# A decoder layer's two norms: GpSimd takes the residual and the bias, ScalarE the normalising, and the first norm's statistics are formed in another way

## The chip, the cores and the metric

The kernel runs on one core of a Trainium2 chip. The engines are called PE (TensorE, the matrix engine; PEld is its loading of weights), DVE (VectorE), ACT (ScalarE), POOL (GpSimd) and SP (SyncE, which here only issues transfers). The metric is the device time in microseconds (us) of one execution; the median of three runs is quoted.

## The reference, cut to what matters

One layer: a token mixer, a residual with a norm, a mixture of experts, a residual with a norm. There are T = 2048 tokens of D = 1024 features. Only the two norms and the sum of the experts matter here:

```
x = layer_norm(ALPHA * x + g1 * (mixed @ w_out), ln_mix_g, ln_mix_b)     # first norm
h = x * (1 + sc2) + sh2
y = routed_experts(h) + swiglu(h, sh_w1, sh_w3, sh_w2)                   # 64 experts and a shared one
x = layer_norm(ALPHA * x + g2 * y, ln_ffn_g, ln_ffn_b)                   # second norm, the output

layer_norm(x, g, b): (x - mean) * rsqrt(mean((x - mean)^2) + 1e-5) * g + b     # per token
```

## The kernel before, in words

Tokens lie on the 128 partitions, so a block is 128 tokens by 1024 features in float32, and there are 16 blocks. Matrix products are made of three products of split operands (high and low part). The instructions of each engine run in the order that a planner (a list scheduler with priorities and assumed costs) wrote down when the kernel was built; an engine never passes over a waiting instruction. DMA issues of one engine wait in the same way, in the order of its queue.

**The first norm** (phase_c, L1755 to L1985). For each of 16 blocks PE multiplies the mixer's output with w_out into two PSUM tiles of 512 columns (48 matmuls, L1836). DVE forms r = ALPHA * x + product from each half (L1837) and the half's mean and variance sums (bn_stats, L1840). layer_norm_hat (L1988) joins the two (bn_aggr, L1996), makes the reciprocal root with small DVE instructions (rsqrt, L711 to L716: two integer steps and three Newton steps of three instructions) and has ACT write (r - mean) * rstd (L2004). DVE then makes h2 (L1845, L1849) and x1, the normed stream, already multiplied by ALPHA (L1851, L1852); both go to HBM. PE transposes h2 (L1860), ACT copies it out (L1861), PE forms the router's scores (L1865), and DVE picks the experts.

**The experts and the last stage** (moe_phase). First the shared expert's output for blocks 0 to 5 is written to a buffer acc in HBM; then the routed experts add their outputs to acc by indirect transfers that POOL issues (L2166). When the last of them has landed, the last stage runs: for blocks 6 to 15, in four units of two blocks and two of one, PE computes the shared expert (hidden, L2112 and L2093, and back, L2129). finish (L2353) does one block per step. sums (L2344) loads x1 into y (L2347) and acc into a (L2349), both on SP's queue, and DVE multiplies a by g2 (L2350). back first adds y to the PSUM tile by a matmul with the identity matrix (L2126, two halves per block). DVE then reads the PSUM tile, adds a, and sums the row on the way (L2371). Blocks 0 to 5 need no matmul: in each of the first six steps one of them is taken along, and DVE adds y and a in two halves (L2366).

**The second norm** (norm, L2320) works on one or two blocks at a time: DVE the mean (L2327), ACT the sum of squares (L2329), DVE the variance (L2332) and rsqrt, then per block two instructions of DVE, (y - mean) * ln_g (L2339) and * rstd + ln_b (L2340), and the transfer to the output (L2341, SP's queue). The tiles `y` come from a ring of 8, `a`, the loaded h2 and the scratch of the squares from a ring of 6 (xg).

The lines of the second norm that the change touches:

```
V.scalar_tensor_tensor(y[:, hs], y[:, hs], mean[:, i:i + 1], ln[0][:, hs], op0=ALU.add, op1=ALU.mult)
V.scalar_tensor_tensor(y[:, hs], y[:, hs], rs[:, i:i + 1], ln[1][:, hs], op0=ALU.mult, op1=ALU.add)
nc.sync.dma_start(out[rows, hs], y[:, hs])
```

Of the kernel before, what the change touches and what calls it, by code (L numbers as in the profile page):

```python
# [6 lines left out]
F32 = mybir.dt.float32  # L7
# [5 lines left out]
AF = mybir.ActivationFunctionType  # L13
ALU = mybir.AluOpType
AX = mybir.AxisListType
PSUM = bass.MemoryType.PSUM
P = 128
T = 2048
D = 1024
KT = D // P  # L20
NT = T // P
CH = 512
# [6 lines left out]
ALPHA = 2.0 ** 0.25  # L29
# [1725 lines left out]
def phase_c(tc, A, g, S, mixT, modrow, C):  # L1755


    nc = tc.nc
    V, G, ACT, PE = nc.vector, nc.gpsimd, nc.scalar, nc.tensor
    woH, woL = C.wo  # L1760
    with ExitStack() as es:
# [3 lines left out]
        wk = pool("c_wk", 2)  # L1765
# [52 lines left out]
        def tile_(t, h2T):  # L1818
            t0 = t * P
            parts = C.first if t == 0 else []  # L1820
            load = mixed(nc, S, mx_ if t % 2 else C.mx, t, parts, G if t == 1 else nc.sync, V)
            if t:
                next(load)
            x = xp.tile([P, D], F32, name="x")
            nc.sync.dma_start(x, A["x"][0, t0:t0 + P, :])
            if t:
                next(load)
            mH, mL = parts
            yield
            r = rp.tile([P, D], F32, name="r")  # L1830
            for n in range(2):
                ps = C.pp.tile([P, CH], F32, name="po")
                sl = slice(n * 512, (n + 1) * 512)
                for k in range(KT):
                    for i, (a_, b_) in enumerate(((mH, woH), (mH, woL), (mL, woH))):
                        PE.matmul(ps, lhsT=a_[:, k, :], rhs=b_[:, k, sl], start=(k == 0 and i == 0), stop=(k == KT - 1 and i == 2))  # L1836
                V.scalar_tensor_tensor(r[:, sl], x[:, sl], ALPHA, ps, op0=ALU.mult, op1=ALU.add)  # L1837
                if n == 0:
                    st = sm.tile([P, 2, 6], F32, name="lnst", bufs=2)
                V.bn_stats(out=st[:, n, :], in_=r[:, sl])  # L1840
                yield
            xh = layer_norm_hat(tc, sm, r, r, st=st)
            yield
            h2 = wk.tile([P, D], F32, name="h2")
            V.tensor_tensor(h2, xh, bc["sc2"], op=ALU.mult)  # L1845

            hp = wk.tile([P, D], F32, name="h2p", bufs=3)
            cut = lambda a: a.rearrange("p (q k) -> p q k", k=KT)
            V.tensor_tensor(hp.rearrange("p (k q) -> p q k", k=KT), cut(h2), cut(bc["sh2"]), op=ALU.add)  # L1849
            h2 = hp  # L1850
            V.tensor_tensor(xh, xh, lng, op=ALU.mult)  # L1851
            V.tensor_tensor(xh, xh, lnb, op=ALU.add)  # L1852
            nc.sync.dma_start(S["x1"][t0:t0 + P, :], xh)
            nc.sync.dma_start(S["h2"][t0:t0 + P, 0:D], h2)
            yield
            hT = wk.tile([P, KT, P], F32, name="hT")
            for n in range(2):
                ps = pt.tile([P, CH], F32, name="tr")
                for k in range(4):
                    PE.transpose(ps[:, k * P:(k + 1) * P], h2[:, (4 * n + k) * P:(4 * n + k + 1) * P], g.ident)  # L1860
                ACT.activation(hT[:, 4 * n:4 * n + 4, :].rearrange("p a b -> p (a b)"), ps, AF.Copy)  # L1861
            yield
            ps = pr.tile([P, CH], F32, name="rt")
            for k in range(KT):
                PE.matmul(ps[:, 0:NE], lhsT=hT[:, k, :], rhs=rw[:, k, :], start=(k == 0), stop=(k == KT - 1))  # L1865
            ACT.activation(h2T, ps[:, 0:NE], AF.Sigmoid)
            yield
# [117 lines left out]
        rank_experts(tc, g, S, cnt_e, sm, pr)  # L1985


def layer_norm_hat(tc, sm, out, r, parts=1, st=None):  # L1988

    nc = tc.nc  # L1990
    if st is None:
        st = sm.tile([P, 2, 6], F32, name="lnst")
        for n in range(2):
            nc.vector.bn_stats(out=st[:, n, :], in_=r[:, n * 512:(n + 1) * 512])
    mv = sm.tile([P, 2], F32, name="lnmv")
    nc.vector.bn_aggr(out=mv, in_=st)  # L1996
    va = sm.tile([P, 1], F32, name="lnva")
    nc.vector.tensor_scalar(va, mv[:, 1:2], 1e-5, None, op0=ALU.add)
    y = rsqrt(nc, sm, va, [P, 1], None, "ln")
    nb = sm.tile([P, 1], F32, name="lnnb")  # L2000
    nc.vector.scalar_tensor_tensor(nb, mv[:, 0:1], -1.0, y, op0=ALU.mult, op1=ALU.mult)
    for i in range(parts):
        c = slice(i * D // parts, (i + 1) * D // parts)
        nc.scalar.activation(out[:, c], r[:, c], AF.Identity, bias=nb, scale=y)  # L2004
    return out
NEAR = 4
NEAR2 = 5
# [6 lines left out]
def moe_phase(tc, A, g, S, modrow, out):  # L2014
    nc = tc.nc
    V, G, ACT, PE = nc.vector, nc.gpsimd, nc.scalar, nc.tensor
    with ExitStack() as es:
# [100 lines left out]
                V.tensor_tensor(s[:, 0:n], s[:, 0:n], ps[1][:, 0:n], op=ALU.mult)  # L2118
                split_to(nc, gH[:, m, 0:n], gL[:, m, 0:n], s[:, 0:n])

        def back(w, gH, gL, c, n, more=None):

            for h in range(2):
                ps = py_.tile([P, CH], F32, name="py")
                if more is not None:
                    PE.matmul(ps, lhsT=g.ident, rhs=more[:, h * CH:(h + 1) * CH], start=True, stop=False)  # L2126
                for m in range(2):
                    for j, (a, b) in enumerate(TERMS):
                        PE.matmul(ps[:n], lhsT=(gH, gL)[a][:, m, c:c + n], rhs=w[2][b][:, m, h * CH:(h + 1) * CH],  # L2129
                                  start=(more is None and m == 0 and j == 0), stop=(m == 1 and j == 2))  # L2130
                yield h, ps

        def gather(idx, eid, c0, n):
# [186 lines left out]
        def norm(blocks):  # L2320


            n = len(blocks)
            mean = sm.tile([P, 2], F32, name="lnmean")[:, 0:n]
            sq = sm.tile([P, 2], F32, name="lnsq")[:, 0:n]
            for i, (rows, y, su) in enumerate(blocks):
                V.tensor_scalar(mean[:, i:i + 1], su[:, 0:1], su[:, 1:2], -1.0 / D, op0=ALU.add, op1=ALU.mult)  # L2327
                junk = xg.tile([P, HC], F32, name="x")[:, 0:D]
                ACT.activation(junk, y, AF.Square, bias=mean[:, i:i + 1], accum_out=sq[:, i:i + 1])  # L2329
            yield  # L2330
            va = sm.tile([P, 2], F32, name="lnva")[:, 0:n]
            V.tensor_scalar(va, sq, 1.0 / D, 1e-5, op0=ALU.mult, op1=ALU.add)  # L2332
            rs = rsqrt(nc, sm, va, [P, n], None, f"ln{n}")
            yield
            for i, (rows, y, su) in enumerate(blocks):
                parts = 2 if rows.stop == T else 1
                for q in range(parts):
                    hs = slice(q * D // parts, (q + 1) * D // parts)
                    V.scalar_tensor_tensor(y[:, hs], y[:, hs], mean[:, i:i + 1], ln[0][:, hs], op0=ALU.add, op1=ALU.mult)  # L2339
                    V.scalar_tensor_tensor(y[:, hs], y[:, hs], rs[:, i:i + 1], ln[1][:, hs], op0=ALU.mult, op1=ALU.add)  # L2340
                    nc.sync.dma_start(out[rows, hs], y[:, hs])  # L2341
                yield

        def sums(rows):  # L2344

            y = buffer()
            nc.sync.dma_start(y, S["x1"][rows, :])  # L2347
            a = xg.tile([P, HC], F32, name="x")[:, 0:D]
            nc.sync.dma_start(a, S["acc"][rows, :])  # L2349
            V.tensor_tensor(a, a, g2b, op=ALU.mult)  # L2350
            return y, a, sm.tile([P, 2], F32, name="lnsu", bufs=8)

        def finish(w, c0, n, g_, more):  # L2353
            done = []
            for c in range(0, n, P):
                rows = slice(c0 + c, c0 + c + P)
                y, a, su = sums(rows)
                norms()
                blocks_left[0] -= 1
                early = []  # L2360
                for _ in range(-(-len(more) // (blocks_left[0] + 1))):
                    r2 = slice(more[-1], more.pop() + P)
                    y2, a2, su2 = sums(r2)
                    for q in range(2):
                        hs = slice(q * CH, (q + 1) * CH)
                        V.scalar_tensor_tensor(y2[:, hs], y2[:, hs], 1.0, a2[:, hs], op0=ALU.mult, op1=ALU.add,  # L2366
                                               accum_out=su2[:, q:q + 1])
                    done.append((r2, y2, su2))
                for q, ps in back(w, g_[0], g_[1], c, P, y):
                    hs = slice(q * CH, (q + 1) * CH)  # L2370
                    V.scalar_tensor_tensor(y[:, hs], ps, 1.0, a[:, hs], op0=ALU.mult, op1=ALU.add, accum_out=su[:, q:q + 1])  # L2371
                done.append((rows, y, su))
                if len(done) >= 2 or c + P == n:
                    for i in range(0, len(done), 2):
                        under_way.append(norm(done[i:i + 2]))
                        next(under_way[-1])
                    done = []
                yield
# [115 lines left out]
```

## Time and profile before

| what | us |
|---|---|
| median of three runs (lowest, highest) | 3731.58 (3721.93, 3741.07) |
| the profiled execution, its own time | 3729.63 |
| its span, first to last instruction | 3727.9 |
| the first norm's steady stretch (from 1840 to 2010) | 170 |
| the last stage, from the first L2350 to the last DVE instruction | 102.5 |

In the rows below a time at the head of a line is counted from the span's start; the second figure is the instruction's duration. "x2" behind a row of a timeline means that two neighbours were merged. An instruction's record can begin before its predecessor on the same engine has ended, so the distance of two starts is the better measure of what one costs in a full queue. `w` and `x` are the program's names for the tiles that hold y and a; `wraw` is the tile with ln_g or ln_b, and `py`, `tr`, `p` and `po` are PSUM tiles.

### The profile page before, as it was taken

To read this page: it belongs to the slowest core of one execution; us is meant where nothing else is said; L and a number is where in the kernel's file an instruction comes from. 1 tells how busy PE (TensorE), PEld (TensorE's weight loads), DVE (VectorE), ACT (ScalarE), POOL (GpSimd) and SP (SyncE) were. 2 spreads that over 40 slices of the span, in tenths; PEclk is the share of its full clock that TensorE was granted. 3 is DMA by queue.
4 is the path that set the end of the run, shared out by engine and by line. 5 is a ranking of instruction groups with operands and counts; after the bars stand their busy time and mean duration, and the time that the engine had idled before them with its cause. 6 is when DMAs were issued, how large, how long until landed. Compare 5 with 4: busy or idle time off the path is not lost. (4 is left out here: it accounts for less than half of the span.)

```text
span 3727.9 us, 64046 instructions
## 1 busy us (share of the span) xinstructions
PE 3439.3 (92%) x23084; PEld 2985.7 (80%) x23084; DVE 2640.9 (71%) x6951; ACT 1962.2 (53%) x3471; POOL 881.8 (24%) x817
## 2 busy tenths in 40 slices
PE   7899999799999879999898799999999999999998
PEld 5677777688888767778787798998888888888996
DVE  6555899888888678888799545555556555556659
ACT  4243656355555567767322355555555555556642
POOL 1000000322223155543000022332223322232210
PEclk9999999899999889999999899999999999999999
DMA  7756466400000132222543478888889888888986
GB/s 251 232 199 221 150 211 226 162 26 25 20 24 18 30 105 79 84 66 78 170 149 140 146 206 232 242 232 233 244 244 242 244 236 234 236 234 256 290 237 215
DMA packets 276235, 640.38 MB, mean 172 GB/s; under 512 B 34428, under 2 KB 115364, under 8 KB 275784
## 3 DMA queue, kind: packets, MB, share of 16 engines
q1 hardware_dynamic: 231760, 481.09, 38.6%
q0 software_dynamic: 40832, 150.32, 18.2%
q10 hardware_dynamic: 3320, 4.83, 0.4%
q8 instruction: 183, 3.00, 0.3%
q14 instruction: 140, 1.15, 0.1%
HBM read 467.14 MB, written 169.00 MB: 171 GB/s over the span
## 5 line engine op out<-in xcount | busy, mean ns | idle before, releaser
L2112 PE MATMUL p<-hH,w 128*128 128x256 f32 (+8 forms) x4352 | 875.1, 289 | 9.3 <-DVE w L2060 6.6
L2112 PEld LDWEIGHTS p<-hH,w 128*128 128x128 f32 x4352 | 707.4, 191 | 18.9 <-DVE w L2060 6.9
L2060 DVE TENSOR_TENSOR w<-wraw,w 128x1024 fp32r<-128x1024 f32 x396 | 474.7, 1223 | 293.2 <-ACT w L2059 278.9
L2112 PE MATMUL p<-hL,w 128*128 128x256 f32 (+8 forms) x2176 | 617.2, 284 | 0.7 <-DVE hL L65 0.7
L2059 ACT ACTIVATE w<-wraw 128x1024 fp32r<-128x1024 f32 x396 | 406.2, 1054 | 234.5 <-DMA wraw<-in_exp_w_dram 112.2
L2166 POOL DMA_INDIRECT scratch_acc<-y,idx x157 | 262.3, 1671 | 782.6 <-ACT y L2165 312.8
L2129 PE MATMUL py<-w,gH 128*128 128x512 f32 (+5 forms) x1384 | 441.8, 401 | 2.0 <-ACT gH L62 1.6
L2112 PEld LDWEIGHTS p<-hL,w 128*128 128x128 f32 x2176 | 416.4, 191 | 6.5 <-DVE hL L65 0.9
L343 PE MATMUL pj<-hTH,w 128*128 128x512 f32 x1152 | 376.6, 402 | 16.6 <-ACT w L202 10.8
L65 DVE TENSOR_TENSOR hL<-tr,hH 128x512 fp32r<-128x512 f32 (+7 forms) x346 | 213.2, 627 | 210.8 <-ACT hH L62 197.6
L2129 PEld LDWEIGHTS py<-w,gH 128*128 128x128 f32 (+5 forms) x1384 | 236.6, 178 | 68.4 <-issue 8.1
L2165 ACT ACTIVATE y<-py,gt 128x512 f32<-128x512 f32 (+5 forms) x314 | 213.6, 683 | 145.9 <-PE py L2129 132.8
L343 PEld LDWEIGHTS pj<-hTH,w 128*128 128x128 f32 x1152 | 220.5, 193 | 70.8 <-ACT w L202 13.8
L62 ACT ACTIVATE hH<-tr 128x512 fp32r<-128x512 f32 (+7 forms) x346 | 184.3, 545 | 176.1 <-PE tr L2072 156.5
L2129 PE MATMUL py<-w,gL 128*128 128x512 f32 (+5 forms) x692 | 273.9, 396 | 0.6 <-DVE gL L65 0.5
L2140 POOL DMA_INDIRECT x<-scratch_h,idx x157 | 162.9, 1038 | 333.0 <-DVE L L2182 80.3
L343 PE MATMUL pj<-hTL,w 128*128 128x512 f32 x576 | 230.9, 401 | 0.0
L2072 PE MATMUL tr<-ident,x 128*128 128x128 f32 (+5 forms) x1384 | 191.9, 265 | 35.0 <-issue 17.9
L2072 PEld LDWEIGHTS tr<-ident,x 128*128 128x128 f32 (+5 forms) x1384 | 149.6, 140 | 46.0 <-issue 30.5
L2129 PEld LDWEIGHTS py<-w,gL 128*128 128x128 f32 (+5 forms) x692 | 122.9, 178 | 39.1 <-DVE gL L65 1.8
L2093 PE MATMUL p<-w,hH 128*128 128x256 f32 (+2 forms) x736 | 141.8, 289 | 0.0
L343 PEld LDWEIGHTS pj<-hTL,w 128*128 128x128 f32 x576 | 111.5, 194 | 23.5 <-issue 0.9
(626 smaller groups left out, 8152.0 us busy)
## 6 DMA issues: line engine op xcount, KB each, us to landing
wraw<-in_exp_w_dram SPq DMA_DIRECT2D x384, 512.0 KB
w<-scratch_wH SPq DMA_DIRECT2D x57, 512.0 KB
w<-scratch_wL SPq DMA_DIRECT2D x57, 512.0 KB
mw<-in_w_mod_dram SPq DMA_DIRECT2D x48, 512.0 KB
scratch_rw<-po SPq DMA_DIRECT2D x44, 256.0 KB
w<-in_w_in_dram SPq DMA_DIRECT2D x21, 512.0 KB
x<-in_x_dram SPq DMA_DIRECT2D x40, 256.0 KB
scratch_wH<-w SPq DMA_DIRECT2D x19, 512.0 KB
```

The costliest lines, as they stand in the source:

```text
L62: nc.scalar.activation(hi, src, AF.Copy)
L65: (lo_eng or nc.vector).tensor_tensor(lo, src, hi.bitcast(F32), op=ALU.subtract)
L343: nc.tensor.matmul(ps, lhsT=a_[:, k, :], rhs=b_[k], start=(k == 0 and i == 0), stop=(k == KT - 1 and i == 2))
L2059: ACT.activation(wh[:, c], raw, AF.Copy)
L2060: V.tensor_tensor(wl[:, c], raw, wh[:, c].bitcast(F32), op=ALU.subtract)
L2072: PE.transpose(ps[:, k * n:(k + 1) * n], x[0:n, (4 * h + k) * P:(4 * h + k + 1) * P], g.ident[0:n, 0:n])
L2093: PE.matmul(ps[i][:n, 0:256], lhsT=(hH, hL)[a][:, k, 0:n], rhs=w[i][b][:, k, :], start=(k == 0 and j == 0), stop=(k == KT - 1 and j == 2))
L2112: PE.matmul(ps[i][:, 0:n], lhsT=w[i][a][:, k, m * P:(m + 1) * P], rhs=(hH, hL)[b][:, k, 0:n], start=(k == 0 and j == 0), stop=(k == KT - 1 ...
L2129: PE.matmul(ps[:n], lhsT=(gH, gL)[a][:, m, c:c + n], rhs=w[2][b][:, m, h * CH:(h + 1) * CH], start=(more is None and m == 0 and j == 0), s ...
L2140: G.indirect_dma_start(out=x[0:m, :], out_offset=None, in_=S["h2"], in_offset=bass.IndirectOffsetOnAxis(ap=ix[0:m], axis=0))
L2165: ACT.activation(y[:m, hs], ps[:m], AF.Copy, scale=gt[:m])
L2166: G.indirect_dma_start(out=S["acc"], out_offset=bass.IndirectOffsetOnAxis(ap=ix[0:m], axis=0), in_=y[0:m, :], in_offset=None, compute_op=A ...
```

## The change

In the last stage GpSimd adds y (x1) to a after DVE's product with g2. The matmul with the identity is gone. For blocks 0 to 5 ACT copies a to y in two halves and sums on the way. In the norm DVE forms -mean * rstd (nb), ACT writes y * rstd + nb, DVE multiplies by ln_g, and GpSimd adds ln_b, except in blocks 14 and 15, where DVE does. In the first norm the row sums come from L1837 itself, ACT forms the sum of squares of r - mean, and bn_stats and bn_aggr are gone.

```
@@ phase_c, tile_
-                V.scalar_tensor_tensor(r[:, sl], x[:, sl], ALPHA, ps, op0=ALU.mult, op1=ALU.add)
                 if n == 0:
-                    st = sm.tile([P, 2, 6], F32, name="lnst", bufs=2)
-                V.bn_stats(out=st[:, n, :], in_=r[:, sl])
+                    su = sm.tile([P, 2], F32, name="lnsu", bufs=2)
+                V.scalar_tensor_tensor(r[:, sl], x[:, sl], ALPHA, ps, op0=ALU.mult, op1=ALU.add, accum_out=su[:, n:n + 1])
                 yield
-            xh = layer_norm_hat(tc, sm, r, r, st=st)
-            yield
             h2 = wk.tile([P, D], F32, name="h2")
+            xh = layer_norm_hat(tc, sm, r, r, su, h2)
+            yield
@@ layer_norm_hat(tc, sm, out, r, su, junk)
-    nc.vector.bn_aggr(out=mv, in_=st)
+    mean = sm.tile([P, 1], F32, name="lnmean")
+    nc.vector.tensor_scalar(mean, su[:, 0:1], su[:, 1:2], -1.0 / D, op0=ALU.add, op1=ALU.mult)
     va = sm.tile([P, 1], F32, name="lnva")
-    nc.vector.tensor_scalar(va, mv[:, 1:2], 1e-5, None, op0=ALU.add)
+    nc.scalar.activation(junk, r, AF.Square, bias=mean, accum_out=va)
+    nc.vector.tensor_scalar(va, va, 1.0 / D, 1e-5, op0=ALU.mult, op1=ALU.add)
...
@@ back
-                if more is not None:
-                    PE.matmul(ps, lhsT=g.ident, rhs=more[:, h * CH:(h + 1) * CH], start=True, stop=False)
@@ norm
+            nb = sm.tile([P, 2], F32, name="lnnb")[:, 0:n]
+            V.tensor_tensor(nb, mean, rs, op=ALU.mult)
             yield
             for i, (rows, y, su) in enumerate(blocks):
+                ACT.activation(y, y, AF.Identity, bias=nb[:, i:i + 1], scale=rs[:, i:i + 1])
+                ended = rows.stop > T - 2 * P
                 parts = 2 if rows.stop == T else 1
                 for q in range(parts):
                     hs = slice(q * D // parts, (q + 1) * D // parts)
-                    V.scalar_tensor_tensor(y[:, hs], y[:, hs], mean[:, i:i + 1], ln[0][:, hs], op0=ALU.add, op1=ALU.mult)
-                    V.scalar_tensor_tensor(y[:, hs], y[:, hs], rs[:, i:i + 1], ln[1][:, hs], op0=ALU.mult, op1=ALU.add)
+                    V.tensor_tensor(y[:, hs], y[:, hs], ln[0][:, hs], op=ALU.mult)
+                    (V if ended else G).tensor_tensor(y[:, hs], y[:, hs], ln[1][:, hs], op=ALU.add)
                     nc.sync.dma_start(out[rows, hs], y[:, hs])
@@ sums
             V.tensor_tensor(a, a, g2b, op=ALU.mult)
+            G.tensor_tensor(a, a, y, op=ALU.add)
@@ finish
                     for q in range(2):
                         hs = slice(q * CH, (q + 1) * CH)
-                        V.scalar_tensor_tensor(y2[:, hs], y2[:, hs], 1.0, a2[:, hs], op0=ALU.mult, op1=ALU.add,
-                                               accum_out=su2[:, q:q + 1])
+                        ACT.activation(y2[:, hs], a2[:, hs], AF.Identity, accum_out=su2[:, q:q + 1])
                     done.append((r2, y2, su2))
-                for q, ps in back(w, g_[0], g_[1], c, P, y):
+                for q, ps in back(w, g_[0], g_[1], c, P):
```

## Rows read from the trace of the kernel before

**Rows 1.** Busy time by stretch: the stretch, its length, then the busy time and the count of instructions of PE, PEld, DVE, ACT and POOL, the granted TensorE clock (1.00 is full speed), the DMA share and GB/s. The first line is the first norm's steady stretch, the second the last stage without its end.

```profile
1840.00:2010.00 170.00, 170.00 (x907) 145.15 (x906) 159.66 (x509) 44.19 (x62) 2.75 (x4) 1.00 0.42 142
...
3621.30:3705.00 83.70, 77.65 (x468) 64.03 (x467) 82.67 (x207) 26.94 (x52) 0.00 (x0) 1.00 0.64 219
```

**Rows 2.** The chain of work that ended last, its end: start, duration, what.

```profile
3723.09 0.75 DVE w L2340
3723.84 0.66 DVEq L2490
```

**Rows 3.** DVE's groups of instructions in the last stage (3612 to the end): line, operation, output<-inputs, shapes, count, then busy time and mean ns of one.

```profile
L2350 DVE TENSOR_TENSOR x<-x,g2b 128x1024 f32<-128x1024 f32 x16 | 19.4, 1218 | 7.8 <-DMA x<-scratch_acc 7.8
L2339 DVE SCALAR_TENSOR_TENSOR w<-w,lnmean,wraw 128x1024 f32<-128x1024 f32 x15 | 19.2, 1279 | 0.5 <-ACT x L2329 0.5
...
L2371 DVE SCALAR_TENSOR_TENSOR w<-py,x 128x512 f32<-128x512 f32 x20 | 13.6, 684 | 0.0
L2366 DVE SCALAR_TENSOR_TENSOR w<-w,x 128x512 f32<-128x512 f32 x12 | 8.2, 686 | 0.0
...
L716 DVE SCALAR_TENSOR_TENSOR ln2y<-ln2a,ln2y 128x2 f32<-128x2 f32 x21 | 3.3, 156 | 0.2
...
L65 DVE TENSOR_TENSOR gL<-s,gH 128x256 fp32r<-128x256 f32 x6 | 2.5, 417 | 0.0
...
L716 DVE SCALAR_TENSOR_TENSOR ln1y<-ln1a,ln1y 128x1 f32<-128x1 f32 x6 | 0.9, 158 | 0.2
```

**Rows 4.** DVE's timeline in the last stage: its beginning, a pair of L2340, and three neighbours in a full queue.

```profile
3621.30 2.36 DVE L2350 TENSOR_TENSOR x<-x,g2b 128x1024 f32<-128x1024 f32 x2 [7.79 <-DMA x<-scratch_acc]
...
3651.39 2.47 DVE L2340 SCALAR_TENSOR_TENSOR w<-w,ln2y,wraw 128x1024 f32<-128x1024 f32 x2
...
3660.31 0.15 DVE L715 TENSOR_TENSOR ln2a<-ln2a,lnva 128x2 f32<-128x2 f32 x1
3660.39 0.68 DVE L2366 SCALAR_TENSOR_TENSOR w<-w,x 128x512 f32<-128x512 f32 x1
...
3661.07 0.68 DVE L2371 SCALAR_TENSOR_TENSOR w<-py,x 128x512 f32<-128x512 f32 x1
```

**Rows 5.** PE's timeline: a routed half block without the identity matmul begins at 3602.61 and the next at 3603.98; a half block of the last stage with it begins at 3613.41 and the next at 3615.67; the last instruction of the stage.

```profile
3602.61 0.62 PE L2129 MATMUL py<-w,gH 128*128 128x512 f32 x2
...
3603.98 0.62 PE L2129 MATMUL py<-w,gH 128*128 128x512 f32 x2
...
3613.41 1.02 PE L2126 MATMUL py<-w,ident 128*128 128x512 f32 x2
...
3615.67 1.02 PE L2126 MATMUL py<-w,ident 128*128 128x512 f32 x2
...
3713.77 0.39 PE L2129 MATMUL py<-w,gL 128*128 128x512 f32 x1
```

**Rows 6.** POOL's groups with two inputs of 128x1024 float32, over the whole span (columns as in rows 3). None of them adds whole tiles of the last stage; both are subtractions.

```profile
L65 POOL TENSOR_TENSOR mwl<-mw,mwh 128x1024 fp32r<-128x1024 f32 x32 | 77.3, 2414 | 37.7 <-ACT mwh L62 35.0 <-PE w L1446 2.8
...
L859 POOL TENSOR_TENSOR ya<-ra 128x1024 f32<-128x1024 f32 x4 | 8.2, 2042 | 4.5 <-DMA ra<-scratch_rw 4.5
```

**Rows 7.** Timelines of POOL and DVE side by side, in earlier stages where both work. First the same pair of instructions twice (L919 and L933), then a small DVE instruction beside a POOL one, then a DVE instruction with one input (`w`) in PSUM beside a POOL subtraction.

```profile
1108.00 1.77 POOL L919 TENSOR_TENSOR kka<-kk,sga 128x512 f32<-128x512 f32 x1 [16.03 <-DVE kk L916]
1107.95 0.69 DVE L933 SCALAR_TENSOR_TENSOR ar<-kk,csr 128x512 f32<-128x512 f32 x1
...
1153.45 1.27 POOL L919 TENSOR_TENSOR kka<-kk,sga 128x512 f32<-128x512 f32 x1 [14.76 <-DVE kk L916]
1153.49 1.77 DVE L933 SCALAR_TENSOR_TENSOR ar<-kk,csr 128x512 f32<-128x512 f32 x1
...
1318.91 1.27 POOL L1235 TENSOR_TENSOR ckL<-ck,ckH 128x512 fp32r<-128x512 f32 x1 [0.44 <-DVE hra L714]
1318.96 1.23 DVE L715 TENSOR_TENSOR hra<-hra,hrx 128x8 f32<-128x8 f32 x1
...
1345.95 2.38 POOL L65 TENSOR_TENSOR mwl<-mw,mwh 128x1024 fp32r<-128x1024 f32 x1 [2.76 <-PE w L1446]
1347.10 0.67 DVE L1542 TENSOR_TENSOR mrow<-mrow,w 2x512 f32<-2x512 f32 x1
```

**Rows 8.** ACT's groups: the squares of the second norm with their accumulator's reading (columns as in rows 3).

```profile
L2329 ACT ACTIVATE x<-w,lnmean 128x1024 f32<-128x1024 f32 x16 | 18.3, 1145 | 48.4 <-DVE lnmean L2327 26.0 <-issue 19.4 <-DVE ln2y L716 3.0
L2329 ACT ACTIVATION_READ_ACCUMULATOR x<-w,lnmean 128x1 f32 x16 | 3.0, 186 | 0.0
```

**Rows 9.** The first norm: PE's transposes of two blocks that follow each other; the statistics' instructions (shortest, median, longest ns); ACT's normalising of the last block and DVE's wait beside it.

```profile
1916.32 1.03 PE L1860 MATMUL tr<-ident,h2p 128*128 128x128 f32 x8
...
1929.93 1.03 PE L1860 MATMUL tr<-ident,h2p 128*128 128x128 f32 x8
...
L1840 DVE BATCH_NORM_STATS2 lnst<-r x32: 672/686/696, 1809.2 to 2024.3; 128x6 f32<-128x512 f32 x32
...
2030.84 1.23 ACT L2004 ACTIVATE r<-r,lnnb,lny 128x1024 f32<-128x1024 f32 x1
...
2033.94 0.29 DVE L1888 TENSOR_TENSOR gt<-gs 128x128 f32<-128x128 f32 x1 [2.58 <-DMA scratch_h<-gt]
```

**Rows 10.** SP's queue in the last stage: an output and the next load of acc, in order.

```profile
3666.51 0.34 SPq L2341 DMA_DIRECT2D out_dram<-w  x1
3666.89 0.43 SPq L2349 DMA_DIRECT2D x<-scratch_acc  x1
```

More of the change, by code (lines that the diff above doesn't have):

```diff
@@ L1836, in tile_ @@
                         PE.matmul(ps, lhsT=a_[:, k, :], rhs=b_[:, k, sl], start=(k == 0 and i == 0), stop=(k == KT - 1 and i == 2))
-                V.scalar_tensor_tensor(r[:, sl], x[:, sl], ALPHA, ps, op0=ALU.mult, op1=ALU.add)
                 if n == 0:
-                    st = sm.tile([P, 2, 6], F32, name="lnst", bufs=2)
-                V.bn_stats(out=st[:, n, :], in_=r[:, sl])
+                    su = sm.tile([P, 2], F32, name="lnsu", bufs=2)
+                V.scalar_tensor_tensor(r[:, sl], x[:, sl], ALPHA, ps, op0=ALU.mult, op1=ALU.add, accum_out=su[:, n:n + 1])
                 yield
-            xh = layer_norm_hat(tc, sm, r, r, st=st)
+            h2 = wk.tile([P, D], F32, name="h2")
+            xh = layer_norm_hat(tc, sm, r, r, su, h2)
             yield
-            h2 = wk.tile([P, D], F32, name="h2")
             V.tensor_tensor(h2, xh, bc["sc2"], op=ALU.mult)
@@ L1985, in phase_c, with layer_norm_hat @@
         rank_experts(tc, g, S, cnt_e, sm, pr)
-def layer_norm_hat(tc, sm, out, r, parts=1, st=None):
+def layer_norm_hat(tc, sm, out, r, su, junk):
     nc = tc.nc
[L1991 to L1995, printed above, removed]
-    nc.vector.bn_aggr(out=mv, in_=st)
+    mean = sm.tile([P, 1], F32, name="lnmean")
+    nc.vector.tensor_scalar(mean, su[:, 0:1], su[:, 1:2], -1.0 / D, op0=ALU.add, op1=ALU.mult)
     va = sm.tile([P, 1], F32, name="lnva")
-    nc.vector.tensor_scalar(va, mv[:, 1:2], 1e-5, None, op0=ALU.add)
+    nc.scalar.activation(junk, r, AF.Square, bias=mean, accum_out=va)
+    nc.vector.tensor_scalar(va, va, 1.0 / D, 1e-5, op0=ALU.mult, op1=ALU.add)
     y = rsqrt(nc, sm, va, [P, 1], None, "ln")
     nb = sm.tile([P, 1], F32, name="lnnb")
[L2001 to L2004, printed above, removed]
+    nc.vector.tensor_tensor(nb, mean, y, op=ALU.mult)
+    nc.scalar.activation(out, r, AF.Identity, bias=nb, scale=y)
     return out
@@ L2119, in hidden, with back @@
                 split_to(nc, gH[:, m, 0:n], gL[:, m, 0:n], s[:, 0:n])
-        def back(w, gH, gL, c, n, more=None):
+        def back(w, gH, gL, c, n):
             for h in range(2):
                 ps = py_.tile([P, CH], F32, name="py")
-                if more is not None:
-                    PE.matmul(ps, lhsT=g.ident, rhs=more[:, h * CH:(h + 1) * CH], start=True, stop=False)
                 for m in range(2):
@@ L2129, in back @@
                         PE.matmul(ps[:n], lhsT=(gH, gL)[a][:, m, c:c + n], rhs=w[2][b][:, m, h * CH:(h + 1) * CH],
-                                  start=(more is None and m == 0 and j == 0), stop=(m == 1 and j == 2))
+                                  start=(m == 0 and j == 0), stop=(m == 1 and j == 2))
                 yield h, ps
```

## The prediction

> **What bounds the kernel now.** I read the busy time by stretch first. In the first norm's steady stretch PE is busy for all of its 170 us while DVE is busy for 160; in the last stage DVE is busy for 82.67 us of 83.70 and PE for 77.65 [rows 1]. So one engine sets each stretch: PE the first norm, DVE the last stage, with PE close behind. The chain that ended last confirms this at the end: it is DVE's last halves of L2340, and behind the last, which starts at 3723.84, come the output transfer and the end of the span at 3727.9, a tail of 4.1 us [rows 2]. DVE's groups and timeline then say what its 102.5 us from 3621.30 to 3723.84 consist of [rows 3, 4]. POOL has no instruction in that stretch [rows 1], which makes it look free; whether it is free is read from earlier stages, where both engines work at once [rows 7].
>
> **The first norm: nothing.** DVE loses two bn_stats of 0.69 per block [rows 9] and a few small instructions change; ACT gains one square with accumulator, 1.15 + 0.19 [rows 8], where it is busy for 44 of 170 us [rows 1]. But blocks follow each other on PE at 1929.93 - 1916.32 = 13.61 us [rows 9], and PE has no gap. Less work on DVE therefore brings nothing there, and 1.34 us more delay inside a block is covered by the block behind it. At the stretch's end the chain of the last block gets longer: 1.34 of square against 1.4 of bn_stats and their joining, within 2 us either way. DVE's wait of 2.58 us for a transfer, right behind the last normalising, could hide it [rows 9]. I take 0, with -2 and +2 as ends.
>
> **The last stage, engine by engine.** DVE: neighbours start 2.47 - 1.27 = 1.20 us apart in the pair of L2340, and 2.36 - 1.22 = 1.14 apart in the pair of L2350 [rows 3, 4]. Gone are 16 blocks by two instructions at 1.20, 38.4, and twelve L2366 at 0.68, 8.2. New are 16 multiplications by ln_g at L2350's 1.14, 18.2, two additions of ln_b, 2.3, and nine nb at about 0.1, 0.9. Net: -25.2, which leaves 77.3 of the 102.5. PE: a half block with the identity matmul takes 3615.67 - 3613.41 = 2.26, without it 3603.98 - 3602.61 = 1.37 [rows 5]; 20 halves give -17.8. ACT gets 16 normalisings at 1.23 [rows 9], 19.7, and twelve copies of halves, which the trace lacks; half the square's 1.15 and its accumulator's 0.19 [rows 8] make 0.77, at most 1.34, so 9 to 16 us. Its 26.94 busy us of 83.70 [rows 1] become some 56 to 63 of about 100: hidden, though a copy of gH that PE wants may stand one such instruction late.
>
> GpSimd gets 30 instructions with two inputs of 128x1024: 16 additions of y, and of the bias in 14 blocks. The nearest rows are its subtractions of the same shape: L65, 2.41 in the mean and 2.38 where nothing is in its way, and L859, 2.04 [rows 6, 7]. By 2.38 that is 71 us, less than the stage lasts. By duration alone it would fit.
>
> **What the two engines do to each other.** The same two instructions stand side by side twice [rows 7]. Where DVE's L933 begins first it takes 0.69, and GpSimd's L919 takes 1.77 where 1.27 is normal. Where L919 begins first it takes its 1.27, and L933 takes 1.77. One waits out the other. In the second pair L919 ends at 1154.72; L933 ends at 1155.26, and its own 0.69 would have begun at 1154.57, 0.15 before that. The size of the DVE instruction is no help: L715 on 128x8, which otherwise takes some 0.16 as its like does [rows 3], takes 1.23 beside L1235, again from 0.15 before its end. L1542, with one input in PSUM, takes a plain 0.67 in the middle of a GpSimd subtraction [rows 7]. So I count a common resource: each GpSimd instruction takes it for its duration less 0.15, and each DVE instruction with two inputs in SBUF for its own.
>
> The Trainium skill has this as a rule ("SBUF — State Buffer", section "Who interferes with whom"): GpSimd's ports are DVE's second pair, and the pair is an exclusive lock. It speaks against this change; the trace agrees, with 1.77 for 0.69, save for the 0.15 us by which DVE starts earlier. The skill's "GPSIMD Engine Reference" (section 3.1) lists 2.6 cycles an element for such an addition; an estimate from its 4497 ns for 2048 columns is 2.25 for one here, which would make the sum below 4 us shorter than L65's 2.38 does.
>
> The sum from 3621.30: GpSimd 30 x 2.23 = 66.9. DVE with two SBUF inputs: 16 x 1.14 for g2 (18.2), 18.2 for ln_g, 2.3 for the last biases, six gL at 0.42 less the overlap of 0.07 (2.1), and the small ones: 21 two-column and 6 one-column executions of each of L714 to L716, 81 in all, and nine nb, 90 x 0.155 = 14.0 [rows 3]. Together 54.8, and 121.7 with GpSimd's. In the last block's chain the resource idles for two L2371 (1.37), the mean (0.2), the square (1.34) and the normalising (1.23), 4.1; then comes the tail of 4.1. The end lies at 3621.3 + 121.7 + 8.2 = 3751.2, 23.3 after 3727.9. DVE's other work, 77.3 - 54.8 = 22.5 us, mostly L2371, can run while GpSimd holds the resource, but only when it is at the head of DVE's queue: as soon as a held instruction stands there, the evacuations behind it wait too, and PE for their PSUM tiles. Each of the ten dependent steps of rsqrt can meet a new addition. I leave a sixth of the 22.5 uncovered, 3.8. Total +27.
>
> Ends of this: the low one with additions at 2.04 (1.89 each, 56.7) and small instructions at the 0.08 by which they follow in a full queue (3660.31 to 3660.39 [rows 4]; 7.2 in place of 14.0): 56.7 + 48.0 + 8.2 = 112.9, ending at 3734.2, +6. The high one with none of the 22.5 covered: 3773.7, +46. On SP's queue the output transfer L2341 now waits for GpSimd's bias addition, and the next load of acc (L2349) stands right behind it [rows 10], so a late addition delays a later block's a as well; `a` also stays in its ring until GpSimd's sum has been read. I put this into the upper end. Taking the identity matmul away gives PE 17.8 us that nothing can use while evacuations come late.
>
> The profiled execution's own time is 3729.63, 1.95 below the median of 3731.58; I carry differences over to the median: 3731.6 + 27 is about 3758.
>
> **Rivals.** *A, faster:* GpSimd's additions fall where DVE reads PSUM or waits, and hold nobody. DVE then has 77.3 us and PE sets the stage: its last matmul at 3713.77 + 0.39 moves to 3696.4; evacuation 0.7, mean 0.2, square 1.34, ten small steps 2, normalising 1.23 and two halves with ln_g and bias at about 0.6 bring the end to 3702.7, the tail to 3706.8: -21, 3711. For it speak POOL's empty stage and L1542; against it, that 54.8 of DVE's 77.3 us have two SBUF inputs, so 67 us of additions cannot fit into the remaining 22.5. The Trainium skill's "Perfetto Trace Analysis" (section "Identifying the Most-Contended Engine") would have the engine with the highest occupancy relieved first, which is this hope; the trace agrees that it is DVE. *B, break-even:* the low prices, 3738, or down to 3722 if the order lets additions overlap DVE's waits as well. For it: the 2.04 of L859, and that small instructions in a full queue cost half their record. Against: L65's 2.38 has 32 executions behind it, L859 four. *C, much slower:* small steps of rsqrt and the evacuations behind them each wait for an addition, nothing is covered: 3777. It decides from the point where GpSimd always has a ready addition queued; for it the 1.23 of L715, against it that the planner can set other work between.
>
> **How the numbers follow.** Chances: forecast (3750 to 3768) 0.49, A 0.10, B 0.28, C 0.13. What a measurement of this kernel can tell from no change is about 0.5%, 18.7 us, so "same" reaches from 3713 to 3750. Slower is the forecast and C, 0.62; same B, 0.28; faster A, 0.10. The range 3722 to 3777 holds the low prices of B and the high end, and leaves out A and a little beyond C.
>
> **What would show it.** In the profile after, L714 to L716 of the last stage should have executions of over 1 us beside GpSimd additions of about 2.4, DVE's busy time should grow or stay near full although its own work fell by a quarter, PE should wait for py from L2371, and the first norm's transposes should still be 13.6 us apart. The prediction is wrong if small DVE instructions stay at 0.16 beside an addition, if additions take far less than 2.04, or if the first norm's stretch changes length by more than 2 us.

## The result and the profile after

The changed kernel takes 3774.22 us in the median of four runs, the kernel before in the same comparison 3729.91. The ratio is 1.0113 (95% interval 1.0092 to 1.0135), so it is slower by some 42 us. The forecast was +27, with 3722 to 3777 as its range: the direction and the range held, the size was too small by a third of what came.

The two profiled executions differ by 3774.3 - 3727.9 = 46.4 us of span, and that can be laid out by place. The first norm's end brings the experts' first matmul forward by 7.1 us (2064.8 to 2057.7, shown further down). From there to the first L2350, now L2346, it is 1556.5 us before and 1561.5 after, 5.0 more in code that is the same; over the kernels below that distance lies between 1549 and 1567 us (one kernel that adds transfers there is the exception). The six kernels with the last stage's arithmetic of before lie at 1549 to 1558, the seven with a changed one at 1555 to 1567, with one trace each; whether the change has a part in the 5.0 is not shown. The last stage, from that instruction to DVE's last, grows from 103.2 to 151.6 us, 48.4. The 102.5 us in the table ahead of the prediction end at 3723.84, before DVE's last instruction has ended. Here the stage ends with it, in both kernels the second of two halves:

```profile
3723.09 1.41 DVE L2340 SCALAR_TENSOR_TENSOR w<-w,ln1y,wraw 128x512 f32<-128x512 f32 x2
```

```profile
3769.46 1.29 DVE L2336 TENSOR_TENSOR w<-w,wraw 128x512 f32<-128x512 f32 x2
```

Because of the scatter between, the experiments are read by the length of their last stage, and by their whole time only where the interval carries it. In the four kernels that leave the last stage as it was the length repeats within 0.3 us; of each changed stage there is one trace.

First the busy time by stretch of the kernel after, the first norm's steady part and the last stage (columns as in [rows 1]):

```profile
1840.00:2010.00 170.00, 170.00 (x907) 145.26 (x906) 152.35 (x518) 59.31 (x87) 2.74 (x4) 1.00 0.43 145
3619.16:3770.20 151.04, 89.84 (x468) 76.72 (x466) 120.28 (x235) 55.89 (x97) 79.37 (x30) 0.76 0.40 141
```

In the last stage DVE was busy for 82.67 of 83.70 us before [rows 1]. Now it is busy for 120.28 of 151.04, though its own work was cut by a quarter: its records have become longer, and it also idles for 31 us. Who holds it shows in the groups, DVE's first and then GpSimd's (columns as in [rows 3]). In the kernel after, L2346 is the product with g2, L2347 GpSimd's addition of y, L2363 ACT's copy for the early blocks, L2367 the evacuation; in the norm L2319 is the mean, L2321 ACT's square, L2324 the variance, L2330 ACT's normalising, L2335 the product with ln_g and L2336 the addition of ln_b.

```profile
L2335 DVE TENSOR_TENSOR w<-w,wraw 128x1024 f32<-128x1024 f32 (+1 forms) x17 | 28.9, 1702 | 4.4 <-ACT w L2330 4.2
L2346 DVE TENSOR_TENSOR x<-x,g2b 128x1024 f32<-128x1024 f32 x16 | 26.8, 1680 | 9.0 <-DMA x<-scratch_acc 9.0
L2367 DVE SCALAR_TENSOR_TENSOR w<-py,x 128x512 f32<-128x512 f32 x20 | 12.9, 680 | 4.5 <-POOL x L2347 4.5
L2324 DVE TENSOR_SCALAR lnva<-lnsq 128x2 f32<-128x2 f32 (+1 forms) x9 | 8.4, 929 | 7.3 <-ACT x L2321 7.2
L716 DVE SCALAR_TENSOR_TENSOR ln2y<-ln2a,ln2y 128x2 f32<-128x2 f32 x21 | 7.6, 364 | 0.7
...
L715 DVE TENSOR_TENSOR ln2a<-ln2a,lnva 128x2 f32<-128x2 f32 x21 | 3.4, 161 | 0.7
L714 DVE SCALAR_TENSOR_TENSOR ln2a<-ln2y 128x2 f32<-128x2 f32 x21 | 3.4, 160 | 0.6
```

```profile
L2347 POOL TENSOR_TENSOR x<-x,w 128x1024 f32<-128x1024 f32 x16 | 44.5, 2790 | 46.4 <-issue 18.4 <-DVE x L2346 12.9 <-PE p L2106 9.5
L2336 POOL TENSOR_TENSOR w<-w,wraw 128x1024 f32<-128x1024 f32 x14 | 35.1, 2507 | 22.7 <-DVE w L2335 22.7
```

The product with g2 took 1218 ns in the mean before [rows 3] and takes 1680 now. L2367 reads PSUM and stays at 680 (684 before, [rows 3]). GpSimd's additions take 2.34 to 2.40 us where they are free and 3.1 to 3.4 in the nine executions that met a whole-tile product of DVE already running; with these L2347's mean is 2.79. So both sides wait. Of the steps of rsqrt few are held here: L716 on two columns goes from 156 ns [rows 3] to 364 by two executions of 2.23 and 2.35 us, while L714 and L715 stay at 160 and 161. Four moments from the timelines of the kernel after show which DVE instructions are held:

```profile
3646.04 2.38 POOL L2336 TENSOR_TENSOR w<-w,wraw 128x1024 f32<-128x1024 f32 x1 [2.09 <-DVE w L2335]
3646.21 2.23 DVE L711 TENSOR_SCALAR ln2i<-lnva 128x2 int32<-128x2 int32 x1
...
3657.01 5.83 POOL L2347 TENSOR_TENSOR x<-x,w 128x1024 f32<-128x1024 f32 x2
...
3661.15 0.68 DVE L2367 SCALAR_TENSOR_TENSOR w<-py,x 128x512 f32<-128x512 f32 x1
...
3751.76 2.38 POOL L2336 TENSOR_TENSOR w<-w,wraw 128x1024 f32<-128x1024 f32 x1 [1.16 <-DVE w L2335]
...
3753.30 0.15 DVE L711 TENSOR_SCALAR ln1i<-lnva 128x1 int32<-128x1 int32 x1
...
3753.68 0.48 DVE L714 SCALAR_TENSOR_TENSOR ln1a<-ln1y 128x1 f32<-128x1 f32 x1
```

L711 on two columns takes 2.23 us, to the end of the addition; the same L711 on one column passes beside another addition in 0.15. L714 has two inputs in SBUF and is held even on one column, for the 0.46 us that the addition still has. L2367 runs through. What DVE waits for in the stage is in the waits (in all, times, longest):

```profile
DVE x L2346 <- DMA x<-scratch_acc: 9.0, 4, 6.7
DVE lnmean L2319 <- ACT w L2363: 8.7, 5, 2.4
DVE lnva L2324 <- ACT x L2321: 7.2, 7, 1.5
DVE w L2367 <- POOL x L2347: 4.5, 2, 2.3
DVE w L2335 <- ACT w L2330: 4.2, 6, 1.4
```

The 6.7 us lie ahead of the stage, the other 2.3 of the first row in it. The other four rows are new: before, DVE waited in the stage for nothing but 0.5 us for a square [rows 3]. 20 us of them are waits for ACT. DVE waits for PE nowhere in this stage.

### The profile page after: what moved, and what is told of

It is laid out like the page before. It is cut to its first block, busy times and chain, and to the rows that moved or that the text cites. A ratio compares the mean times of both kernels' runs of the same rounds, so it can differ in the third digit from the quotient of the medians.

```text
span 3774.3 us, 64055 instructions
## 1 busy us (share of the span) xinstructions
PE 3447.3 (91%) x23044; PEld 2995.3 (79%) x23044; DVE 2645.2 (70%) x6922; ACT 2008.3 (53%) x3543; POOL 954.4 (25%) x847
## 5 line engine op out<-in xcount | busy, mean ns | idle before, releaser
L2121 PE MATMUL py<-w,gH 128*128 128x512 f32 (+5 forms) x1384 | 455.2, 411 | 40.3 <-DVE w L2367 37.6
L65 DVE TENSOR_TENSOR hL<-tr,hH 128x512 fp32r<-128x512 f32 (+7 forms) x346 | 213.2, 627 | 218.6 <-ACT hH L62 217.8
L2121 PEld LDWEIGHTS py<-w,gH 128*128 128x128 f32 (+5 forms) x1384 | 245.0, 185 | 105.3 <-DVE w L2367 30.4
L2121 PE MATMUL py<-w,gL 128*128 128x512 f32 (+5 forms) x692 | 282.3, 408 | 1.4 <-DVE gL L65 1.4
```

What stands on the lines that cost most here:

```text
L65: (lo_eng or nc.vector).tensor_tensor(lo, src, hi.bitcast(F32), op=ALU.subtract)
```

## The experiments

Two theories are weighed. By the lock theory a GpSimd addition and a DVE instruction with two inputs in SBUF exclude each other; by the chain theory the stage is longer because each block goes through more engines, one after the other. Each kernel is named by its edit. "Stage" is the length from the first product with g2 to DVE's last instruction.

| kernel | whole time against before (95% interval) | stage, us | DVE busy in it | GpSimd busy in it |
|---|---|---|---|---|
| before | 1 | 103.2 | 101.3 | 0 |
| changed | 1.0113 (1.0092, 1.0135) | 151.6 | 120.8 | 79.4 |
| first norm alone | 0.9963 (0.9940, 0.9987) | 103.4 | 101.4 | 0 |
| the same again, five rounds | 0.9972 (0.9957, 0.9987) | 103.4 | 101.4 | 0 |
| that + unused bn_stats | 0.9995 (0.9981, 1.0009) | 103.5 | 101.4 | 0 |
| first norm + ACT normalises | 1.0027 (1.0011, 1.0044) | 116.6 | 102.7 | 0 |
| that + ln_b on GpSimd | 1.0072 (1.0047, 1.0097) | 134.0 | 114.1 | 38.3 |
| changed, ln_b on DVE | 1.0063 (1.0038, 1.0087) | 140.4 | 120.7 | 39.6 |
| changed, y on DVE | 1.0073 (1.0049, 1.0096) | 139.9 | 115.9 | 37.9 |
| changed, both on DVE | 1.0067 (1.0040, 1.0093) | 126.4 | 113.8 | 0 |
| changed, blocks 0 to 5 as before | 1.0095 (1.0060, 1.0130) | 149.3 | 123.1 | 63.8 |
| before + useless GpSimd additions | 1.0169 (1.0139, 1.0200) | 174.3 | 154.2 | 78.3 |
| before + useless ACT copies | 1.0001 (0.9984, 1.0018) | 103.7 | 101.6 | 0 |
| before, ln_b added by the transfer | 1.0064 (1.0046, 1.0083) | 110.2 | 88.1 | 12.1, transfers' issue |

**Useless additions and their control.** GpSimd gets 30 additions whose result nobody reads:

```
             V.tensor_tensor(a, a, g2b, op=ALU.mult)
+            G.tensor_tensor(dump, a, y, op=ALU.add)
...
+                    if rows.stop <= T - 2 * P:
+                        G.tensor_tensor(dump, y, ln[1], op=ALU.add)
```

> The kernel before, unchanged, and beside it on GpSimd 30 additions of 128x1024 float32 whose result nobody reads: 16 that read a and y after DVE's product with g2, 14 that read the finished y and ln_b. No instruction of the kernel waits for them but the reuse of their inputs' buffers. Lock theory: DVE's instructions with two inputs in SBUF take 79.9 us of the stage before, the additions 66.9, together 146.8 with DVE's remaining 22.6 us mostly beside them: the stage grows from 102.5 to 147 to 160, 3773 to 3790 us, and small instructions of rsqrt show 1 to 2.3 us. Chain theory: nothing is put into any block's chain, so within 5 us of the kernel before.

The control has `ACT.activation(dump, a, AF.Copy)` and the like in their place:

> The control to the useless additions: 30 instructions in the same places, on the same inputs, but on ACT (a copy of 128x1024 each). Lock theory: ACT shares nothing with DVE, 30 x 1.15 us beside ACT's 30 busy us of the stage are hidden; within 8 us of the kernel before, what is over 0 being squares and copies of gH that stand behind a useless copy. A loss of 30 us or more would mean that buffers or the order of work, not the lock, make the useless additions costly.

The additions made the stage 174.3 us, 71 longer, more than the 147 to 160 expected (whole time 3802.83, expected 3773 to 3790); the copies made it 103.7. In the groups of the kernel with useless additions (DVE, columns as in [rows 3]) and in one moment of its timeline:

```profile
L2341 DVE SCALAR_TENSOR_TENSOR w<-w,ln2y,wraw 128x1024 f32<-128x1024 f32 x14 | 23.5, 1687 | 0.2
...
L716 DVE SCALAR_TENSOR_TENSOR ln2y<-ln2a,ln2y 128x2 f32<-128x2 f32 x21 | 17.6, 836 | 0.6
L714 DVE SCALAR_TENSOR_TENSOR ln2a<-ln2y 128x2 f32<-128x2 f32 x21 | 17.5, 835 | 0.4
...
L715 DVE TENSOR_TENSOR ln2a<-ln2a,lnva 128x2 f32<-128x2 f32 x21 | 12.8, 609 | 0.4
L2370 DVE SCALAR_TENSOR_TENSOR w<-w,x 128x512 f32<-128x512 f32 x12 | 7.9, 686 | 6.9 <-POOL dump L2354 6.9
```

```profile
3686.39 4.88 POOL L2343 TENSOR_TENSOR dump<-w,wraw 128x1024 f32<-128x1024 f32 x2
...
3686.58 2.22 DVE L715 TENSOR_TENSOR ln2a<-ln2a,lnva 128x2 f32<-128x2 f32 x1
...
3689.03 2.24 DVE L714 SCALAR_TENSOR_TENSOR ln2a<-ln2y 128x2 f32<-128x2 f32 x1
```

L716 goes from 156 ns [rows 3] to 836. Two neighbours of one rsqrt, L715 and L714, each wait for one of two additions that follow each other. This settles the lock: nobody needs these sums, and 52.9 of the 71 us are the same DVE instructions taking longer (busy 154.2 us against 101.3). DVE's idle time grows by 18.3. 9.4 of these are a wait that the edit itself puts there, for y to be read before it is overwritten (6.9 us of L2370 and 2.5 of L2375); the control cannot show this wait, since its copies of a do not read y. Most of the rest are waits for squares (4.9 us, where 0.5 stood before) and for PE (3.5). The time of additions and of DVE's instructions with two SBUF inputs, overlaps counted once over both timelines, is 146.1 us, where 146.8 was expected. What was not foreseen is that 28.2 us stay beside it, more even than the 23.3 us that the stage before has outside such instructions (103.2 - 79.9). In 19.5 of the 28.2 DVE works on other instructions, where it did for 21.4 before: almost none of its other work found its place beside an addition. In 8.7 neither engine works.

**The first norm alone.** The kernel before with the diff's parts of phase_c and layer_norm_hat.

> The kernel before with the first norm of the changed one; the last stage stays as it was. Both theories expect no change: PE has no gap in the first norm's steady stretch. 3726 to 3734 us, transposes 13.6 us apart. If it differs by more than 4 us from the kernel before, the first norm has a part in the 44 us after all.

The time fell, by 0.4%, and the steady stretch is not where: its transposes are 13.6 us apart as before. It is the end of the norm. PE's timeline there, from the last matmul with w_out by the last transposes to the experts' first matmul, first before, then after:

```profile
2018.15 0.39 PE L1836 MATMUL po<-woH,mL 128*128 128x512 f32 x1
...
2037.53 1.94 PE L1860 MATMUL tr<-ident,h2p 128*128 128x128 f32 x8 [6.85 <-DVE h2p L1849]
...
2064.82 0.58 PE L2112 MATMUL p<-hH,w 128*128 128x256 f32 x1
```

```profile
2017.96 0.39 PE L1836 MATMUL po<-woH,mL 128*128 128x512 f32 x1
...
2032.01 1.94 PE L1859 MATMUL tr<-ident,h2p 128*128 128x128 f32 x8 [6.20 <-DVE h2p L1848]
...
2057.72 0.58 PE L2106 MATMUL p<-hH,w 128*128 128x256 f32 x1
```

46.7 us have become 39.8, and 40.0 in the kernel with the first norm alone. To see why, two bn_stats that nobody reads were put back behind L1839:

```
+                st = sm.tile([P, 2, 6], F32, name="lnst", bufs=2) if n == 0 else st
+                V.bn_stats(out=st[:, n, :], in_=r[:, sl])
```

> The kernel with the changed first norm and the last stage of before, and in the first norm again two bn_stats of 0.68 us per block whose result nobody reads. The first norm's change shortened the time from the last matmul with w_out (it starts at 2018.1 us before, 2020.2 with the changed norm) to the experts' first matmul from 46.7 to 40.0 us. Theory of the backlog: DVE, busy for 159.66 us of 170 in the steady stretch of before, is behind PE at its end, and 1.1 us less work per block lets it catch up. Then the useless work brings most of the 46.7 us back: 44 to 48 us, and about 4 to 8 us in the whole time. Theory of the chain: the last block's own chain got shorter or its instructions come in a better order. Then 40 to 42 us.

```profile
2014.49 0.39 PE L1836 MATMUL po<-woH,mL 128*128 128x512 f32 x1
...
2034.65 1.94 PE L1861 MATMUL tr<-ident,h2p 128*128 128x128 f32 x8 [9.46 <-DVE h2p L1850]
...
2062.00 0.58 PE L2108 MATMUL p<-hH,w 128*128 128x256 f32 x1
```

With them it is 47.5 us, and the whole time is that of before (0.9995). So the gain is DVE's backlog. DVE works in the steady stretch for 159.66 us before [rows 1], for 152.35 after and for 160.33 with the unused bn_stats, and what it is behind by must be done after PE's last matmul. The wait of 2.58 us for scratch_h<-gt [rows 9] belongs to it: in the runs without bn_stats the same instruction does not wait, with the unused ones it waits 2.54.

The kernel with the first norm alone was run once more, as the fastest:

> The kernel with the changed first norm alone, once more, as the fastest candidate: the first time 0.9963 of the kernel before, with 6.7 us of the gain seen in the first norm's tail and the rest in the routed experts' stretch, whose code is the same. If only the tail counts, the ratio is 0.998 (-7 us); at 0.9963 or less the experts' stretch has a part in it.

0.9972, with an interval that holds both -7 us (0.998) and the first 0.9963. That the experts' stretch gains anything is not shown.

**GpSimd's two additions, one and both taken back.** In the changed kernel `G.tensor_tensor` became `V.tensor_tensor` for ln_b, for y, and for both.

> The changed kernel with ln_b added by DVE in all blocks; GpSimd keeps the 16 additions of y. Lock theory (a GpSimd addition and a DVE instruction with two inputs in SBUF exclude each other): 14 additions less of 2.23 us, 14 instructions more of DVE at 1.14, so the common time falls by 15 us from the 124.0 us that the trace after shows, with the same idle time or a little less: 3752 to 3760 us. Chain theory (the stage is longer because each block goes through more engines, one after the other): nobody in the stage waits for the bias, and DVE gets 16 us more work, so the time stays or grows, 3774 to 3790 us.

> The changed kernel with y added to a by DVE in all 16 blocks; GpSimd keeps the 14 additions of ln_b. Lock theory: 16 additions less of 2.23 us (35.7), 18.2 more on DVE, common time 124.0 - 17.5 = 106.5, idle time 15 to 28: 3744 to 3757 us. Chain theory: 2.4 us of latency less in front of each evacuation and each copy, so it also falls, by the 4.5 + some of the 30.9 us of waits for that addition: 3750 to 3770 us. This run tells the two apart only together with the one that moves the bias.

> The changed kernel with both additions on DVE, none on GpSimd. Lock theory: DVE's own work is 77.3 + 18.2 + 16.0 = 111.5 us, nothing holds it, and with 4 to 10 us of waits for ACT the stage takes 116 to 122 us where the changed one takes 151.6: 3738 to 3746 us. Chain theory: the waits for ACT's copies, squares and normalising stay at the 28 us of the changed kernel: 139 us, 3760 to 3764 us.

Moving ln_b to DVE shortened the stage by 11.2 us although DVE got 16 us more work, which the chain theory excluded. Moving y did 11.7, both did 25.2. But with no GpSimd at all the stage is 126.4, above the 116 to 122 of the lock theory and far below the 139 of the other: DVE still idles for 12.6 us, 10.7 more than before. Each theory had a half. In the traces, moving both additions to GpSimd takes the time of additions and of DVE's instructions with two SBUF inputs from 89.3 to 124.0 us, and what stays beside it falls from 37.1 to 27.6: together the 25.2.

The whole times do not resolve this. They are 3760.68 us with ln_b moved, 3762.72 with y and 3759.72 with both, where the lock theory had at most 3760, 3757 and 3746; the third lies a little below the chain theory's 3760 to 3764. Their ratios, 1.0063 to 1.0073, lie within each other's intervals, although the third stage is 13.5 to 14 us shorter. So the 25.2 us are shown by the stage alone.

**The early blocks as before.** Their additions and sums go back to DVE, without ACT's copies.

> The changed kernel with blocks 0 to 5 summed on DVE as before (two instructions that add and sum the halves), without GpSimd's addition and ACT's copies for these six. Lock theory: common time falls by 6 x 2.23 - 12 x 0.69 = 5.1 us, and the 8.7 us in which DVE waits for ACT's copies go, partly to other waits: 3760 to 3769 us. Chain theory: the 30.9 us in which ACT waits for GpSimd's additions to copy are the cost, most of them go: 3745 to 3760 us.

The stage fell by only 2.3 us, less than either theory said, and the whole time, 3775.66, did not fall. ACT's 30.9 us of waits for these additions were hardly a cost, and DVE's 8.7 us of waits for the copies were given back elsewhere: it waits 9.2 us for squares, 6.7 for GpSimd's sums and 2.3 for PE, where the changed kernel has 7.2, 4.5 and none.

**Normalising on ACT, by itself, and then with ln_b on GpSimd.** From the kernel with the first norm alone:

```
+                ACT.activation(y, y, AF.Identity, bias=nb[:, i:i + 1], scale=rs[:, i:i + 1])
...
+                    V.tensor_tensor(y[:, hs], y[:, hs], ln[0][:, hs], op=ALU.mult)
+                    V.tensor_tensor(y[:, hs], y[:, hs], ln[1][:, hs], op=ALU.add)
```

> The kernel with the changed first norm, and in the last stage of before only the normalising on ACT: DVE multiplies by ln_g and adds ln_b, the identity matmul stays, GpSimd adds nothing. DVE's work falls by 16 x 2 x (1.20 - 1.14) = 1.9 us and grows by 0.9 for nb. If only work counts, the stage stays at 103.4 us (102 to 104). If the detour through ACT makes DVE wait as in the changed kernel without GpSimd's additions (12.6 us idle), 105 to 114 us. The whole time goes with the stage, from 3716 to 3729 us.

> The same, with ln_b of blocks 0 to 13 added by GpSimd; nobody waits for these additions but the output transfers. Lock theory: DVE's instructions with two inputs in SBUF fall from 79.9 by 38.4 and rise by 18.2 + 2.3 + 1 to 63, GpSimd takes 14 x 2.23 = 31.2, together 94.2, and the 28 to 32 us in which all runs with GpSimd leave the common resource idle: 122 to 126 us, 10 to 20 longer than with the bias on DVE. Theory without a lock: DVE has 16 us less work, and the stage is at or below the one with the bias on DVE, no less than PE's 100 us.

The first has a stage of 116.6 us, longer than both expectations, where DVE's work grew by 1.3: the detour through ACT costs 13.2. DVE's waits in its stage:

```profile
DVE x L2347 <- DMA x<-scratch_acc: 8.0, 2, 6.3
DVE lnva L2326 <- ACT x L2323: 6.2, 5, 1.6
DVE w L2336 <- ACT w L2332: 3.5, 5, 1.4
```

Two rows, for the square and for the normalising, make 9.7 us, where 0.5 stood before [rows 3]; the 6.3 lie ahead of the stage. Giving ln_b to GpSimd then took 16 us of work from DVE and made the stage 17.4 us longer, 134.0. The common time came out at 94.1 us, as expected (94.2), the time in which it idles at 40, not 28 to 32. The kernel without GpSimd's additions has 78.2 and 38.5 of these: the additions made the common time 15.9 us longer and left the idle time, most of which was there without them, nearly as it was.

**A candidate.** In the kernel before, ACT normalises blocks 0 to 13 and the output transfer adds ln_b.

> A candidate, from the kernel before (first norm as before): in blocks 0 to 13 ACT normalises, DVE multiplies by ln_g, and ln_b is added by the transfer to the output, which accumulates onto rows filled with ln_b earlier; no GpSimd arithmetic. DVE loses 14 x (2.40 - 1.14) = 17.6 us and gains 7 nb, so it falls to 85; PE with the identity matmul keeps 100.8 and becomes the bound: 3720 to 3730 us. If the accumulating transfers (16 times 0.5 MB read and written on the queue that GpSimd issues) land late, 3735 or more.

It is slower by 0.6%. DVE's work fell to 88.1 us, but it idles for 22.0: 8.3 behind the squares, 8.2 behind loads of acc and 3.2 behind the normalising. The stage also starts late, 1579 us after the experts' first matmul, beyond the 1549 to 1567 of all others; that the added transfers are the cause is likely, but no run separates it.

## Why the prediction was right, and where its size failed

The stage's 48.2 us over the kernel with the first norm alone (151.6 against 103.4) divide by runs, taken in this order: normalising on ACT 13.2 (to 116.6), y added by DVE in place of the identity matmul together with ACT's copies for the early blocks 9.8 (to 126.4), and moving both additions from DVE to GpSimd 25.2 (to 151.6).

- **Bounds.** Right for PE and DVE; POOL's empty stretch was no free capacity, as the rows of earlier stages had said.
- **The lock and its sum.** Right. 121.7 us were worked out; the two timelines of the changed kernel laid on each other give 124.0. Free additions take 2.34 to 2.40, as L65's 2.38 had it. The Trainium skill's figure ("GPSIMD Engine Reference", section 3.1), by which an estimate was 2.25 us, is 0.1 below them. Rival A, that they hold nobody, is excluded by the useless additions.
- **What the common resource idles: the step that failed.** I had 4.1 us for the last block's chain and 3.8 for a sixth of DVE's other work, 7.9; the 151.6 us leave 27.6. Of these DVE works for 11.3 on instructions that need no lock, and in 16.3 neither engine works. Of my 4.1, 1.6 were DVE's (two L2371 and the mean), so I had 5.4 for the first, half of what came, and 2.5 for the second, a sixth. In the useless additions the uncovered part was 28.2, with ACT normalising and ln_b on GpSimd 40. I had priced C, with nothing covered, at +46 and gave it 0.13. The changed kernel's stage came out close to that sum, but by another mechanism: of the 81 executions of L714 to L716 only two took over 1 us, and DVE waits 20 us for ACT. The steps of rsqrt behind additions, which C was built on, stand in the kernel with useless additions, where 19 took over 1 us.
- **ACT hidden.** Its busy time is 55.89 us, and 56 to 63 were forecast, but "hidden" was wrong. I counted only its share of the time. DVE's queue is in order, and where it stands at lnva or at the product with ln_g until ACT is done, nothing behind it runs; the normalising alone showed 13.2 us for that. In the forecast that wait stood once, for the last block.
- **PE.** Its 17.8 us were of no use: it waits for evacuations by L2367, and DVE never waits for it. The granted clock of the stage is 0.76 in the mean, against 0.96 for the same stretch of before; PE was busy for 86.0 of 102.6 us before and is for 89.8 of 151.0 now. The mean mixes two levels: after, the clock was 1.00 (2.4 GHz) from 3630 to 3640, where PE was busy for 9.07 us, and 0.50 (1.2 GHz) from 3760 to 3770, where it had no instruction.
- **SP's queue.** The transfers to the output wait 95.9 us for GpSimd's additions of ln_b, as I had feared, but behind the first load DVE waits only 2.3 us for acc (9.0 - 6.7). It decided little here.
- **First norm at nothing.** Wrong by -7, and by my own sign, a change of more than 2 us, the forecast of this part had failed: I read the steady stretch, where PE sets the pace, and took the stretch's end for one block's chain, within 2 us. The row with 2.58 us of wait, which I took as a cover, was a sign of DVE's backlog and went away with it.
- **Two slips in the sums.** The 4.1 us of tail were read from a row of DVE's queue (DVEq, 3723.84). DVE's last half of L2340 ends at 3724.50, so the tail is 3.4 us and 0.7 stands in the forecast twice. In rival A the terms after 3696.4, with two halves of two instructions at 0.6, end at 3704.3, not at 3702.7. Neither changes the argument.

The sum of my errors has two signs: +22 us in the stage (151.6 against 121.7 + 7.9 = 129.6) and -7 in the first norm. The total error, +42 against +27, looks smaller than the stage's, because the two cancel in part; that the time fell inside the range is in part luck.

## What to carry to other kernels

Before giving work to an idle GpSimd, find one place in the trace where it ran beside DVE instructions with both inputs in SBUF, and add its time to theirs; here 14 additions of 2.4 us cost the stage 17 us while DVE lost 16 us of work. An engine that takes over a step in the middle of another's chain has to be priced by the waits that it puts at the head of an in-order queue, at every round, not by its busy time. Of this change the first norm alone is worth keeping (0.9972), and it pays at the end of its stretch, where the engine that does not set the pace has a backlog to clear.

## What the runs showed of the hardware beyond the forecast

A DVE instruction with one SBUF input can be held as well: L711 and L2324 on two columns took 2.23 and up to 2.19 us beside an addition, while on one column they took 0.15 beside one (for L711 see the rows above). The Trainium skill ("SBUF — State Buffer", section "Who interferes with whom") says that `tensor_scalar` can enter a mode that takes both port pairs; the trace agrees in that these two are of that kind, and no run here separates the mode from the number of columns.

Whichever starts first holds the other, as in [rows 7], and both happen in one stage: GpSimd's L2347 took up to 3.40 us where DVE was there first, DVE's L2346 up to 3.43 where GpSimd was. First a product of DVE with the addition that it holds, then an addition with the product that it holds:

```profile
3733.65 1.21 DVE L2335 TENSOR_TENSOR w<-w,wraw 128x1024 f32<-128x1024 f32 x1
3733.68 3.40 POOL L2347 TENSOR_TENSOR x<-x,w 128x1024 f32<-128x1024 f32 x1 [1.16 <-DVE x L2346]
...
3690.03 3.26 POOL L2347 TENSOR_TENSOR x<-x,w 128x1024 f32<-128x1024 f32 x1 [4.75 <-DVE x L2346]
3690.94 3.43 DVE L2346 TENSOR_TENSOR x<-x,g2b 128x1024 f32<-128x1024 f32 x1
```
